# Sums of the FFN-input weight quarters: accumulating DMAs in DRAM instead of additions on GpSimd

## The chip, the cores and the metric

The kernel runs on one core of a Trainium2 chip. The core has a matrix engine (TensorE, PE in the profile, with its weight loads as PEld), VectorE (DVE), ScalarE (ACT), GpSimd (POOL) and SyncE (SP), which here only issues DMAs, beside 16 DMA engines. Each engine works through its own instructions in order, and engines wait for each other by semaphores. The metric is the time of one execution on the device in microseconds; lower is better. All arrays are float32.

## The reference, cut to what matters

The computation is one decoder block on a sequence of 1024 tokens with 1024 channels: a dilated attention and a causal convolution in parallel, merged by gates, and then a feed-forward part:

```python
h = rms_norm(x, g_pre_mix);  z = h @ w_in            # q, k, v, GLU input, two gates
y_attn = dilated_attention_mixer(q, k, v, ...)
y_conv = conformer_conv_mixer(glu_in, ...)           # GLU, depthwise conv of width 31, LN, swish, product
merged = sigmoid(z_ga) * y_attn + sigmoid(z_gc) * y_conv
x = x + rms_norm(merged @ w_mix_out, g_post_mix)
h = rms_norm(x, g_pre_ffn)
gate, up = split(h @ w_ffn_in)                       # 1024 x (2 x 2816)
x = x + rms_norm((silu(gate) * up) @ w_ffn_out, g_post_ffn)
```

The change concerns the weights of `h @ w_ffn_in`, and the sums of blocks of `h` for the same product.

## The kernel before, in words

**Precision.** Every float32 operand of a product is split into a rounded high part and the remainder. ScalarE writes the high part and VectorE (or GpSimd, where `wsplit` is set to it) the low part: `part` and `both` (L208 the copy, L209 the subtraction), `split` (L1337, L1338), `two_weights.split` (L1897, L1898). A product is three matmuls: high with high, high with low, low with high. In `unit` (L318 to L320) and `prod` (L334 to L336) these are 128 x 512.

**Order.** The program is written out by hand. TensorE's products call `tick` once for every step of the contraction, which is three full-width matmuls. Work for the other engines hangs on these ticks: generators registered with `bg` go on by one step per tick, and a yielded number makes them pause that many ticks; `later` and `when` put single steps on a tick. So the ticks set where an instruction stands in its engine's queue, and the semaphores then set when it runs. An engine whose queue is empty ahead of an instruction runs it early, long before the tick's own time on TensorE.

**Stages.** `start` (L565 to L595) loads x and three weights, normalizes and makes the first products (L629) while the rows arrive. Up to about 100 us come single GLU jobs; up to about 560 us pairs of weight tiles (GLU, gates, queries and keys) with one level of a Strassen-Winograd scheme: seven products for eight, from sums of weight quarters that `quarters` has GpSimd make (L228, L229, L235, L236) and from sums of h's blocks. A pair's weights are loaded at L177 through SyncE, 2 ticks into the pair ahead, and their split begins at tick 18. In the same stages the convolution runs on VectorE (L759), with `phases` (L728) on GpSimd. Values, attention, the merge and the output product follow up to about 1090 us, the FFN input up to about 1500, the FFN output up to the end.

**The FFN-input stage.** The first two of 22 column tiles are plain. The other 20 use a Winograd scheme on two levels. For each tile five products of the outer level are made directly (`("one", m, i)`: A11, S1, S2, S4, S3), and the two others are done for pairs of tiles with a second level, seven half-width products per group of two tiles (`("two", g, n)`, L2150 to L2152); there are ten groups. `line` is the order of all of them on TensorE, and `put` gives each its tick.

The weight sums of a tile are `S1 = A21 + A22`, `S2 = S1 + A11`, `S3 = A11 + A21`, `S4 = S2 + A12`. `one_weights` loads the four quarters of tile m by two DMAs (L1853, L1854), 18 ticks ahead; GpSimd makes the sums in SBUF (L1859, L1860, L1868, L1875); ScalarE and VectorE split them. `two_weights` makes the second level's sums in the same way from the quarter that both levels keep (L1923, L1924, L1928, L1932), four additions a group.

The moving operands of the second level are sums of blocks of h. `fourth_sums` and `eighth_sums` make them, half 0 before and half 1 in the first tile of the stage: two subtractions on GpSimd (L427, L428), the rest on VectorE, splits at L421 and L422, and a store to the DRAM tiles `d_t` (L423). `moving_load` (L1947) reads them back, two 512 KB tiles for each product, ahead of its use; those of products 1 and 5 are kept. Results are spilled to DRAM through L1954 (`spill`) for the FFN output. L2059 to L2070 finish the products of a tile, L2080 to L2095 those of a group; L2050 copies the first product of a tile out of PSUM. All these loads and spills stand in SyncE's one queue, in the order of the program.

Of the kernel before, what the change touches and what calls it, by code (L numbers as in the profile page):

```python
# [18 lines left out]
H = 512  # L19
# [43 lines left out]
class Build:  # L63
# [346 lines left out]
    def eighth_sums(self, e, low, given, dst):  # L410
# [16 lines left out]
        nc.gpsimd.tensor_tensor(t1, b11, b12, op=OP.subtract)  # L427
        nc.gpsimd.tensor_tensor(t3, b22, b12, op=OP.subtract)  # L428
# [1070 lines left out]
def build(ctx, tc, aps):  # L1499
# [39 lines left out]
    B.d_t = {(n, e): B.dram.tile([128, 1024], F32, name=f"dt{n}{e}") for n in range(7) for e in range(2)}  # L1539
    B.d_att = {(g, hp): B.dram.tile([128, T], F32, name=f"datt{g}{hp}") for g in range(3) for hp in range(4)}  # L1540
# [4 lines left out]
    def u_out(j, x):  # L1545
        nc.sync.dma_start(B.d_u[j], x)
        B.un = j + 1

# [24 lines left out]
    qs = B.bg(B.quarter_sums(xs, (h[0][:4], h[0][4:], h[1][4:])))  # L1573
    h = xs = None
# [268 lines left out]
    Wj, Yj, Qj, out2, parts, moving = {}, {}, {}, {}, {}, {}  # L1843
    gadd = nc.gpsimd.tensor_tensor

    def one_weights(m):
# [4 lines left out]
        def load():  # L1851
            st["X"], Yj[m] = B.ring(), B.slot()
            nc.sync.dma_start(st["X"], aps["w_f2"][m, 0])  # L1853
            nc.sync.dma_start(Yj[m], aps["w_f2"][m, 1])  # L1854

        def s12():
            x, y, n = st["X"], Yj[m], B.ring()
            st["N"] = n
            gadd(n[:, L], x[:, R], y[:, R], op=OP.add)  # L1859
            gadd(n[:, R], n[:, L], x[:, L], op=OP.add)  # L1860

        def a11():
            x = B.split(st["X"][:, L], H)
            w["A11"] = x[:, L], x[:, R]

        def s3():
            x = st["X"]
            gadd(x[:, R], x[:, L], x[:, R], op=OP.add)  # L1868

        def split12():  # L1870
            h, l = B.both(st["N"])
            w["S1"], w["S2"] = (h[:, L], l[:, L]), (h[:, R], l[:, R])

        def s4():
            gadd(st["X"][:, L], st.pop("N")[:, R], Yj[m][:, L], op=OP.add)  # L1875
# [8 lines left out]
    def halves(y):  # L1884
        return y.rearrange("p (e k n) -> p k e n", e=2, k=2)
# [4 lines left out]
    def two_weights(g):  # L1890
        a = [2 * g, 2 * g + 1]
        st = {}

        def split(n, x):
# [472 lines left out]
```

## Time and profile before

| | |
|---|---|
| median of 3 runs | 1725.92 us (1725.79 to 1732.4) |
| the profiled execution | 1719.96 us, its span 1717.8 us |
| TensorE busy | 1678.9 us, 98% of the span |
| VectorE, ScalarE, GpSimd busy | 1318.9, 850.3, 693.8 us |
| DMA traffic | 345.32 MB, mean 201 GB/s |
| of it on GpSimd's own queue | 352 packets, 0.18 MB |

Busy time is given per engine and per stretch of the span. A matmul's shown duration overlaps the next one's; the spacing of their starts is what TensorE needs. The lists of waits name an engine's instruction, what released it, and the total, number and longest of such waits. In an operation, `b<-d,b` names the tiles written and read without their numbers. Lines of DMAs give the issue; the landing times are listed apart. The granted clock of TensorE is 1.00 at full speed.

### The profile page before, as it was taken

The numbers are of one execution on the slowest core, as the hardware profiler recorded it, in microseconds if no ns is written. First come the engines' busy times: TensorE is split into PE (matmuls) and PEld (weight loads), VectorE is DVE, ScalarE is ACT, GpSimd is POOL, SyncE is SP. The second block draws the span as 40 slices with busy tenths as digits, with TensorE's granted clock in tenths as the row PEclk, the third lists the DMA queues.
The fourth block names the chain that finished last, engine by engine and source line by source line (L and its number), as shares of the span: only waits on it lengthen the run. The fifth ranks groups of instructions, "written<-read, shape, count | busy, mean of one in ns | idle before, by whom it ended". The sixth has DMA issues, their size and how long they took to land.

```text
span 1717.8 us, 24884 instructions
## 1 busy us (share of the span) xinstructions
PE 1678.9 (98%) x8527; PEld 1415.6 (82%) x8527; DVE 1318.9 (77%) x2238; ACT 850.3 (49%) x1676; POOL 693.8 (40%) x523
## 2 busy tenths in 40 slices
PE   9999999999999999999999999879999999999998
PEld 7788888888888899998888888668888888888886
DVE  6789978889998778788876656857676766777686
ACT  6344343444444688888522467333443344364463
POOL 0017778887885456565101301234434544200000
PEclk9999999999999999999999999989999999999999
DMA  4342434445567897889987424286666656795234
GB/s 165 115 172 90 157 117 141 156 175 180 168 183 205 251 274 219 246 238 273 319 277 260 166 87 172 92 317 247 239 248 232 248 215 228 258 363 163 101 133 153
DMA packets 180762, 345.32 MB, mean 201 GB/s; under 512 B 49185, under 2 KB 82460, under 8 KB 180636
## 3 DMA queue, kind: packets, MB, share of 16 engines
q1 hardware_dynamic: 180140, 343.29, 59.7%
q8 instruction: 67, 1.10, 0.3%
q14 instruction: 59, 0.48, 0.1%
q0 software_dynamic: 352, 0.18, 0.1%
q10 hardware_dynamic: 144, 0.26, 0.0%
HBM read 245.63 MB, written 102.76 MB: 203 GB/s over the span
## 4 chain that ended last, share of the span: by engine, by line
PE 38%; DVE 6%; issue 3%; ACT 3%; DMA 2%; SPq 0%; POOL 0%; DVEq 0%; ACTq 0%; POOLq 0%
PE p L2249 12%; PE p L1749 5%; PE p L334 3%; PE p L335 3%; PE p L336 3%; PE p L318 3%; PE p L319 3%; PE p L320 3%; PE p L2152 2%; PE p L2150 2%; PE p L2151 1%; DVE b L2089 1%; ACT b L208 1%; DVE b L1338 1%; DMA b<-dt 1%
## 5 line engine op out<-in xcount | busy, mean ns | idle before, releaser
L336 PE MATMUL p<-b,b 128*128 128x512 f32 x1044 | 407.7, 391 | 8.4 <-DVE b L209 6.6
L334 PE MATMUL p<-b,b 128*128 128x512 f32 x1044 | 408.2, 391 | 3.6 <-ACT b L2050 3.1
L335 PE MATMUL p<-b,b 128*128 128x512 f32 x1044 | 407.6, 390 | 0.0
L336 PEld LDWEIGHTS p<-b,b 128*128 128x128 f32 x1044 | 196.3, 188 | 53.8 <-DVE b L209 10.3
L334 PEld LDWEIGHTS p<-b,b 128*128 128x128 f32 x1044 | 196.6, 188 | 44.6 <-ACT b L2050 4.0
L335 PEld LDWEIGHTS p<-b,b 128*128 128x128 f32 x1044 | 196.6, 188 | 38.2
L2249 PE MATMUL p<-b,b 128*128 128x512 f32 x924 | 209.6, 389 | 0.0
L2249 PEld LDWEIGHTS p<-b,b 128*128 128x128 f32 x924 | 173.4, 188 | 36.0
L759 DVE SCALAR_TENSOR_TENSOR p<-b,par,p 128x511 f32<-128x511 f32 (+14 forms) x232 | 163.5, 739 | 0.0
L318 PE MATMUL p<-b,b 128*128 128x512 f32 x368 | 146.9, 399 | 0.0
L1017 PE MATMUL p<-b,b 128*128 128x512 f32 x384 | 144.1, 407 | 0.0
L320 PE MATMUL p<-b,b 128*128 128x512 f32 x368 | 143.5, 390 | 0.0
L319 PE MATMUL p<-b,b 128*128 128x512 f32 x368 | 143.5, 390 | 0.0
L209 POOL TENSOR_TENSOR b<-d,b 128x1024 fp32r<-128x1024 f32 x44 | 106.9, 2429 | 79.7 <-ACT b L208 72.4
L1859 POOL TENSOR_TENSOR d<-d,b 128x512 f32<-128x512 f32 x20 | 26.2, 1308 | 233.9 <-DMA b<-w_f 188.6
L208 ACT CAST b<-d 128x1024 fp32r<-128x1024 f32 x86 | 90.2, 1049 | 59.3 <-POOL d L229 55.1
L1338 DVE TENSOR_TENSOR b<-b,b 128x512 fp32r<-128x512 f32 x129 | 94.2, 733 | 21.9 <-ACT b L1337 20.4
L1018 PE MATMUL p<-b,b 128*128 128x256 f32 x384 | 107.7, 280 | 0.0
L1337 ACT CAST b<-b 128x512 fp32r<-128x512 f32 x129 | 79.9, 619 | 47.5 <-PE p L2249 18.1
L1146 ACT ACTIVATE c<-c,stat 128x128 f32<-128x128 f32 (+1 forms) x192 | 85.2, 448 | 13.4 <-DVE stat L1136 11.9
L2150 PE MATMUL p<-b,b 128*128 128x256 f32 x280 | 79.7, 285 | 11.8 <-DMA b<-dt 8.7
L1749 PE MATMUL p<-b,b 128*128 128x512 f32 x384 | 89.4, 391 | 0.0
(271 smaller groups left out, 3591.9 us busy)
## 6 DMA issues: line engine op xcount, KB each, us to landing
b<-dt SPq DMA_DIRECT2D x104, 512.0 KB, 5.4
b<-w_in SPq DMA_DIRECT2D x30, 512.0 KB, 4.9
dk<-c SPq DMA_DIRECT2D x48, 256.0 KB, 4.2
dq<-c SPq DMA_DIRECT2D x48, 256.0 KB, 3.5
b<-dq SPq DMA_DIRECT2D x48, 256.0 KB, 4.8
b<-dk SPq DMA_DIRECT2D x48, 256.0 KB, 7.0
d<-w_in SPq DMA_DIRECT2D x23, 512.0 KB, 4.0
b<-w_fo SPq DMA_DIRECT2D x44, 256.0 KB, 5.4
```

What stands on the lines that cost most here:

```text
L318: nc.tensor.matmul(ps, hi[:, s], a, start=kt == 0, stop=False)
L319: nc.tensor.matmul(ps, hi[:, s], b, start=False, stop=False)
L320: nc.tensor.matmul(ps, lo[:, s], a, start=False, stop=kt == nk - 1)
L334: nc.tensor.matmul(ps, hi[:, s], a, start=first and kt == 0, stop=False, skip_group_check=True)
L335: nc.tensor.matmul(ps, hi[:, s], b, start=False, stop=False, skip_group_check=True)
L336: nc.tensor.matmul(ps, lo[:, s], a, start=False, stop=kt == 3, skip_group_check=True)
L759: nc.vector.scalar_tensor_tensor(A[i][:, j:], src[i][:, :H - j], w[i], A[i][:, j:], op0=OP.mult, op1=OP.add)
L1017: nc.tensor.matmul(ps, a, w, start=kt == 0, stop=kt == KT - 1, skip_group_check=True)
L1338: nc.vector.tensor_tensor(s[:, 512:512 + n], src, f(s[:, :n]), op=OP.subtract)
L1749: nc.tensor.matmul(banks[tt][nh], st, wt[:, nh * H:(nh + 1) * H], start=bool(kt == 0 and a), stop=bool(kt == KT - 1 and b))
L2150: nc.tensor.matmul(o, hi, a, start=new, stop=False, skip_group_check=True)
L2249: nc.tensor.matmul(acc[t], x, y, start=first and e == 0, stop=last and e == 2, skip_group_check=True)
```

## The change

Before the stages with pairs a new generator, `weight_sums`, is registered. It makes all weight sums of both levels in DRAM, for all 20 tiles at once: one DMA copies one operand into the DRAM tile of the sum, a second one adds the other operand to it (`accum_op`). There are eight sums, so 16 DMAs, issued from GpSimd's queue and 45 ticks apart. The four sums of the outer level have 20 x 128 x 512 floats, the four of the inner level half of that.

In the FFN-input stage GpSimd does nothing any more. `one_weights` loads A11 and the four ready sums, each 128 x 512, in two steps; `two_weights` loads each of its seven weights by a DMA of its own, 17 ticks ahead of use and 10 ahead of its split. Both then only split. The host stores the weights as quarters (`w_l1`, `w_l2`) instead of tiles with two quarters each (`w_f2`).

The two subtractions of `eighth_sums` move to VectorE. In the order of the products, the first group's products each come after a later product of tile 2, and the finish of h's sums is called one product earlier; in the last tile the group's product 3 comes one product earlier, and the step that takes its result out of PSUM is held until the tile's last product is done.

```diff
@@ eighth_sums
-        nc.gpsimd.tensor_tensor(t1, b11, b12, op=OP.subtract)
-        nc.gpsimd.tensor_tensor(t3, b22, b12, op=OP.subtract)
+        nc.vector.tensor_tensor(t1, b11, b12, op=OP.subtract)
+        nc.vector.tensor_tensor(t3, b22, b12, op=OP.subtract)
@@ build
+    n1, n2 = (FT - PLAIN) * 128, (FT - PLAIN) * 64
+    B.d_s1 = {n: B.dram.tile([n1, H], F32, name=f"ds{n}") for n in ("S1", "S2", "S3", "S4")}
+    B.d_s2 = {n: B.dram.tile([n2, H], F32, name=f"de{n}") for n in ("s1", "s2", "s3", "s4")}
...
+    def weight_sums():
+        def flat(x):
+            return x.rearrange("(a r) n -> a (r n)", r=4)
+        def raw(x):
+            return x.rearrange("m p n -> (m p) n")
+        add = {"accum_op": OP.add, "max_dma_last_dim": 8192}
+        a11, a12, a21, a22 = (raw(aps["w_l1"][i]) for i in range(4))
+        b11, b12, b21, b22 = (raw(aps["w_l2"][i]) for i in range(4))
+        S, s = B.d_s1, B.d_s2
+        for d, x, y in ((S["S1"], a21, a22), (s["s1"], b21, b22), (S["S2"], S["S1"], a11), (s["s2"], s["s1"], b11),
+                        (S["S3"], a11, a21), (s["s3"], b11, b21), (S["S4"], S["S2"], a12), (s["s4"], s["s2"], b12)):
+            nc.gpsimd.dma_start(flat(d), flat(x))
+            yield 44
+            nc.gpsimd.dma_start(flat(d), flat(y), **add)
+            yield 44
...
     qs = B.bg(B.quarter_sums(xs, (h[0][:4], h[0][4:], h[1][4:])))
+    B.bg(weight_sums())
@@ the order of the products
         if m == 2:
-            after = {0: (0,), 1: (1,), 2: (2, 3), 3: (4, 5), 4: (6,)}
+            after = {1: (0,), 2: (1,), 3: (2, 3), 4: (4, 5, 6)}
...
-            after = {1: (0,), 2: (1,), 3: (2,), 4: (3, 4, 5, 6) if m == FT - PLAIN - 1 else ()}
+            after = {1: (0,), 2: (1,), 3: (2, 3) if m == FT - PLAIN - 1 else (2,), 4: (4, 5, 6) if m == FT - PLAIN - 1 else ()}
@@ one_weights (the loads of w_f2 and the additions s12, s3, s4 are gone)
+        def load(x, name, c):
+            nc.sync.dma_start(x, aps["w_l1"][0, m] if name == "A11" else B.d_s1[name][m * 128:(m + 1) * 128])
+        def load12():
+            st["A11"], st["N"] = B.half(), B.slot()
+            load(st["A11"], "A11", 0)
+            load(st["N"][:, L], "S1", 0)
+            load(st["N"][:, R], "S2", 0)
+        def load34():
+            x = st["X"] = B.slot()
+            load(x[:, L], "S4", 0)
+            load(x[:, R], "S3", 0)
...
-        for n, step in ((-18, load), (-9, s12), (-7, a11), (-5, s3), (-3, split12), (0, s4), (5, split34)):
+        for n, step in ((-19, load12), (-8, a11), (-11, load34), (-4, split12), (4, split34)):
@@ two_weights (the additions s12, s3, s4 are gone)
+        def load(n):
+            x = st[n] = B.half()
+            i = {0: 0, 1: 1, 6: 3}.get(n)
+            nc.sync.dma_start(x, B.d_s2[{2: "s2", 3: "s1", 4: "s3", 5: "s4"}[n]][g * 128:(g + 1) * 128] if i is None
+                              else aps["w_l2"][i, g])
+        def split(n):
+            parts[g, n] = B.split(st.pop(n), H)
         for n in range(7):
+            t = at["two", g, n]
+            when(t - 17, lambda n=n: load(n))
+            when(t - 7, lambda n=n: split(n))
@@ the loop over line
-            if m == 0 and i == 2:
+            if m == 0 and i == 1:
                 B.finish(qs)
...
+            if i == 4 and held:
+                held.pop(3)()
...
-            two_done(g, n, ps)
+            if (g, n) == (GROUPS - 1, 3):
+                held[3] = lambda ps=ps: two_done(g, 3, ps)
+            else:
+                two_done(g, n, ps)
```

More of the change, by code (lines that the diff above doesn't have):

```diff
@@ L1841, in when @@
         B.plan.setdefault(max(tick, B.ticks + 1), []).append(step)
[L1843 to L1844 removed]
+    Wj, Qj, out2, parts, moving = {}, {}, {}, {}, {}
     def one_weights(m):
@@ L2340 @@
     wf = tiles(g["w_ffn_in"][0], 8).reshape(2, FT, 128, 1024)
+    wq = wf[:, PLAIN:].reshape(2, FT - PLAIN, 128, 2, H).transpose(0, 3, 1, 2, 4)
+    w2 = wq[:, 1].reshape(2, -1, 2, 128, 2, 256).transpose(2, 4, 1, 3, 0, 5)
     arrays = {
```

64 lines of the change are left out of this document (4 added, 60 removed).

## The prediction

> **What bounds the kernel now.** First the page, then the busy time by stretch, then the waits of TensorE. The page:
>
> ```profile
> span 1717.8 us, 24884 instructions
> PE 1678.9 (98%) x8527; PEld 1415.6 (82%) x8527; DVE 1318.9 (77%) x2238; ACT 850.3 (49%) x1676; POOL 693.8 (40%) x523
> ```
>
> TensorE is busy 98% and idle 38.9 us (1717.8 - 1678.9). No change that leaves the products alone can gain more than that. The same by stretch; columns are the stretch, its length, busy time with instructions of PE, PEld, DVE, ACT, POOL, then the granted clock, the DMA engines' busy share and GB/s:
>
> ```profile
> 0.00:100.00 100.00, 98.46 (x425) 76.20 (x426) 74.97 (x105) 52.24 (x76) 1.99 (x7) 1.00 0.43 157
> 100.00:560.00 460.00, 459.55 (x2032) 379.27 (x2031) 406.02 (x556) 191.43 (x284) 337.08 (x191) 1.00 0.49 156
> 1090.00:1160.00 70.00, 54.65 (x261) 45.16 (x260) 47.47 (x52) 24.69 (x41) 27.52 (x18) 0.93 0.63 242
> 1160.00:1500.00 340.00, 328.19 (x1777) 281.56 (x1776) 239.24 (x289) 139.16 (x223) 142.72 (x101) 1.00 0.66 241
> ```
>
> From 100 to 560 us (the GLU, gate and query/key pairs) TensorE loses 0.45 us in 460: nothing to win there, only to lose. The FFN-input stage, 1090 to 1500, loses 70 - 54.65 = 15.35 and 340 - 328.19 = 11.81 us, together 27.2. That is the ceiling of what the change can win. What ended those idle times (total us, times, longest):
>
> ```profile
> PE p L2150 <- DMA b<-dt: 8.7, 1, 8.7
> PE p L336 <- DVE b L209: 6.6, 8, 1.6
> PE p L2152 <- DVE b L1898: 3.8, 9, 0.5
> PE p L334 <- ACT b L2050: 3.1, 2, 2.0
> PE p L2150 <- DVE b L2080: 2.0, 1, 2.0
> PE p L336 <- DVE b L1338: 1.9, 1, 1.9
> PE p L2150 <- ACT b L1897: 1.1, 1, 1.1
> ```
>
> One wait of 8.7 us for h's block sums out of DRAM (`d_t`), and many short ones for VectorE, mostly for the low part of the split weights (L209, L1898).
>
> **Part 1: GpSimd's sums leave the FFN stage.** Removed are 4 additions for each of 20 tiles and 4 for each of 10 groups, 120 in all, nearly all in this window's GpSimd time (first row); GpSimd itself waits there for the loaded quarters (second row), so it isn't the bound. What it costs is paid by VectorE. Three rows of the timelines (start, duration), the first two the same operation on VectorE without and beside GpSimd, the third what GpSimd ran:
>
> ```profile
> 1090.00:1500.00 410.00, 170.25 (x118) 0.99 0.65 241
> ...
> POOL d L1859 <- DMA b<-w_f: 188.6, 18, 13.8
> ...
> 1100.57 0.68 DVE L1781 TENSOR_TENSOR c<-c,c 128x512 f32<-128x512 f32 x1
> 1103.44 1.78 DVE L1786 TENSOR_TENSOR c<-c,c 128x512 f32<-128x512 f32 x1
> ...
> 1104.64 1.75 POOL L428 TENSOR_TENSOR c<-b,b 128x512 f32<-128x512 f32 x1
> ```
>
> A VectorE operation with two operands in SBUF takes 1.78 us beside GpSimd and 0.68 alone, so each meeting costs about 1.1. Without the additions the short waits should fall. Of the 27.2 us those for VectorE or ACT are 27.2 - 8.7 = 18.5; 6.6 of these (both waits for L2050 and L1338, and the longest for L209) belong to the stage's first 30 us, 11.9 to the steady part. I take half of each as GpSimd's doing, -3 and -6; bounds 0 and -18.5. The Trainium skill, "SBUF — State Buffer", section "Who interferes with whom", says that a VectorE instruction with two SBUF inputs contends with a GpSimd instruction that reads SBUF; these rows agree, with 1.78 against 0.68 us.
>
> **Part 2: h's block sums on VectorE, and the first group one product later.** `eighth_sums` runs twice, so VectorE gets 4 subtractions more, by L1781's row 4 x 0.68 = 2.7 us, two of them ahead of the stage and two in its start. For the group's first product, the place of the 8.7 us:
>
> ```profile
> 1128.30 0.39 PE L335 MATMUL p<-b,b 128*128 128x512 f32 x1
> 1128.53 0.39 PE L336 MATMUL p<-b,b 128*128 128x512 f32 x1
> 1137.64 0.55 PE L2150 MATMUL p<-b,b 128*128 128x256 f32 x1 [8.72 <-DMA b<-dt]
> 1140.34 0.63 PE L334 MATMUL p<-b,b 128*128 128x512 f32 x1
> 1140.76 0.63 PE L335 MATMUL p<-b,b 128*128 128x512 f32 x1
> ...
> 1131.81 1.63 DVE L2070 TENSOR_TENSOR c<-c,c 128x512 f32<-128x512 f32 x1
> ...
> 1133.88 7.86 SPq L1947 DMA_DIRECT2D b<-dt x12
> ```
>
> Tile 1 ends at 1128.53, but the `dt` loads stand in SyncE's queue behind the spill of the sum at L2070, which ends at 1133.44 (1131.81 + 1.63), so they issue at 1133.88 and the first pair lands 3.6 us later, 1137.5. In the change TensorE first does products 0 and 1 of tile 2: 24 matmuls of 0.23 us (start to start, 1128.30 to 1128.53; 0.227 over many) are 5.4 us, so it comes for the group at 1134.2. With VectorE about 2 us earlier at the spill the pair lands at 1135.5: 1.3 us of wait are left, a gain of 7.4. After the wait matmuls start 0.42 us apart instead of 0.227; some six of these and twelve half-width ones cost 2.3 us, gone too if the wait is short. Part 2 then gives -9.7 + 0.7 (the subtractions, half hidden) = -9; bounds -11 (the wait gone) and 0 (the loads no earlier). The last group's product 3 moves ahead of tile 19's last one; both are in the line anyway: 0, and at worst the 2.0 us of L2150 <- L2080 again.
>
> **Part 3: more loads in the stage.** A tile's two 512 KB loads become five of 256 KB (`A11` and four sums), and seven of 256 KB a group are new. A group of two tiles loaded 4 x 512 KB of weights and 10 x 512 KB of `dt` and spilled 7 x 256 KB, 8.75 MB with 21 issues; now it is 4.25 + 5 + 1.75 = 11 MB with 34. The stage's 0.66 becomes about 0.66 x 11/8.75 = 0.83. Median times to landing:
>
> ```profile
> b<-dt SPq DMA_DIRECT2D x104, 512.0 KB, 5.4
> d<-w_f SPq DMA_DIRECT2D x20, 512.0 KB, 5.2
> b<-w_f SPq DMA_DIRECT2D x20, 512.0 KB, 6.5
> ```
>
> A group's weight is issued 10 ticks ahead of its split, and a tick is three full-width matmuls, 0.68 us: 6.8 us of room against 5.2 to 6.5. Where a load is late, ACT waits with PSUM copies behind it, and the split leaves 7 ticks, 4.8 us, before TensorE asks. 70 such weights, a few late past that: +5, bounds 0 and +12.
>
> **Part 4: the accumulating DMAs beside the first stages.** Sixteen DMAs on GpSimd's queue, one every 45 ticks (30.6 us). Each of S1 to S4 is 20 x 128 x 512 x 4 B = 5.24 MB, copied once and added to once; the halves s1 to s4 are 2.62. No step of any engine waits for them before the FFN stage, but GpSimd issues them in order, and an addition waits for its copy. Their price: a DRAM-to-DRAM copy exists already, `rep`:
>
> ```profile
> 57.14 0.77 SPq L529 DMA_DIRECT2D rep<-line x1
> ...
> 62.00:68.00 6.00, 6.00 (x28) 4.99 (x27) 2.90 (x3) 1.95 (x3) 0.00 (x0) 1.00 0.53 201
> ```
>
> 201 GB/s at a share of 0.53 is 379 GB/s at 1.0, so a large copy is 13.8 us of all engines and a small one 6.9. An addition also reads its target: between 13.8 and twice that, 27.6. All sixteen take between 4 x (13.8 + 6.9) x 2 = 166 and 248 us of engine time in some 490 us whose share is 0.49 already: 0.83 to 1.0.
>
> Now where they land. The first copy waits for nothing, and what stands ahead of it on GpSimd is only the table's load; today GpSimd then sits until 88.98 us:
>
> ```profile
> 1.31 0.64 POOL L516 DMA_DIRECT2D c<-p_tab x1 [0.46 <-issue]
> 88.98 1.03 POOL L728 TENSOR_TENSOR c<-b 128x512 f32<-128x512 f32 x1 [87.03 <-DMA b<-du]
> ...
> 12.95 1.15 ACT L603 ACTIVATE b<-b,gains 128x1024 fp32r<-128x1024 f32 x1 [2.72 <-DMA b<-xT]
> 15.48 0.74 PE L629 MATMUL p<-b,b 128*128 128x512 f32 x2 [0.30 <-DVE b L604]
> ...
> 2.00:21.00 19.00, 18.65 (x70) 12.56 (x69) 10.70 (x14) 13.36 (x22) 0.00 (x0) 1.00 0.96 367
> 21.00:44.00 23.00, 23.00 (x114) 19.34 (x114) 18.87 (x31) 15.03 (x21) 0.00 (x0) 1.00 0.01 4
> ```
>
> So it issues at 2 us, not beside a later stage but into the load of x and the first weights, when the DMA engines are 0.96 busy, and not in the 23 us after it, when they are idle. At 12.95 ACT waits for x, and TensorE is hardly ahead of it (0.30 us idle at 15.48): a late x is late at the end. Lower bound 0, if the loads go first. Shared by bytes, the 3.1 MB up to x's third tile (three of x and three weights, 0.52 each) take at half of 367 GB/s until 19 us instead of 12.9: +6. If each engine does a whole 64 KB row of the copy (80 rows of 16384 floats, by the build) for each 1 to 4 KB row of a load, the loads stand for the 13.8 us of the copy: upper bound. With rows so unequal I take a value near that, +11. The Trainium skill, "DMA: Bandwidth & Descriptors", section "Queues, rings and completion order", says that an engine takes turns between queues packet by packet; by that the result is the upper bound if a long row is one packet, and no row here shows two full queues.
>
> In the pairs a weight has this much room:
>
> ```profile
> 316.66 0.38 SPq L177 DMA_DIRECT2D d<-w_in x1
> 331.61 1.05 ACT L208 CAST b<-d 128x1024 fp32r<-128x1024 f32 x1
> ...
> d<-w_in SPq DMA_DIRECT2D x23, 512.0 KB, 4.0
> ...
> 483.00:560.00 77.00, 76.81 (x345) 62.62 (x344) 68.10 (x83) 34.26 (x51) 50.91 (x28) 1.00 0.67 186
> ```
>
> 14.95 us from issue to split against 4.0 to landing, so 10.9 of slack; behind the split stand ACT's PSUM copies and GpSimd's L209. A copy's 13.8 us leaves at most 3 us of it uncovered, and only when it meets the load. An addition of up to 27.6 us is longer than the slack; shared by bytes it halves the loads' rate, and where the share is 0.67 (483 to 560) the backlog is 0.67 x 27.6 - 13.8 = 5 us, inside the slack. Starved by long rows it is 27.6 - 10.9 = 17 us, for three large additions at worst 50. I take +9, nearer to sharing; bounds 0 and 50.
>
> **The sum.** -3 - 6 - 9 + 5 + 11 + 9 = +7 us. The profiled execution took 1719.96 us (span 1717.8 and 2.16 around it), which gives 1727; the runs' median is 1725.92, 6 above it, so the median of the changed kernel is 1733 by the sum. Since the terms of part 4 reach further up than down and those of part 1 are guesses of one half, I put the forecast at +10: 1736 us.
>
> **Rivals.**
> - Faster: the loads go ahead of the copies. Then part 4 is 0 or little, and -3 - 6 - 9 + 5 = -13 stays: 1713. For it: the FFN stage's 27.2 us are real, and SyncE's loads have 10.9 us of slack in the pairs. Against it: 0.96 share at the start, with TensorE 0.30 us behind the data. It decides when the start loses less than 4 us.
> - Even: sharing by bytes, +6 at the start and +3 in the pairs, against -11 in the FFN stage (-13, with 2 us more of late loads): 1724.
> - GpSimd's queue: an addition waits on GpSimd for its copy; if an addition takes over 61 us, the next small copy behind it is late and GpSimd, 337 of 460 us busy in the pairs, holds L209 for TensorE. At 20 us an instance and three of them: 1786.
> - It doesn't do what it says: the FFN stage is not shortened, because ACT waits for the new loads (+12) as long as VectorE did, while part 4 stays: 1750.
>
> **How the numbers follow.** Chances: the forecast's case (start near the row-by-row bound) 0.40, faster 0.22, even 0.22, GpSimd's queue 0.08, no gain in the stage 0.08. About 0.5%, 8.6 us, is what a measurement can tell from no change. Slower by that: 0.40 less a third that ends within it, with the two last, and a few hundredths of even: 0.45; faster: 0.22 and a part of even, 0.28; within: 0.27. The range leaves out a tenth at each end: 1711 (the faster case in full) to 1768 (half of the queue's case); the forecast's own range is 1726 to 1755.
>
> **What would show it.** At the start: L629's products after 14 us late by 6 to 14 us, with ACT's L603 waiting for xT, and the first copy's bytes in GpSimd's queue from 2 us on; if L603 waits no longer than 2.72, that term is wrong. In the pairs, waits of ACT's L208 for w_in, and of TensorE for ACT. In the FFN stage, no GpSimd time, L2150's wait near 1 us, DVE's L209 waits gone; new waits of ACT for the sums if part 3 counts. The prediction falls if TensorE is not idle in the first 25 us, or if the additions take far over 30 us.

## The result, and the profile after

The changed kernel takes 1816.8 us (median of 4 runs, 1815.41 to 1818.03), the kernel before on the same chip 1729.16 (4 runs, 1725.79 to 1735.01). The ratio is 1.0503 [1.0467, 1.0539]: 5% slower, outside the predicted range of 1711 to 1768. The page of the changed kernel (its profiled execution took 1815.71 us), engines and DMA queues:

```profile
span 1813.9 us, 24918 instructions
PE 1705.7 (94%) x8527; PEld 1430.5 (79%) x8527; DVE 1267.4 (70%) x2242; ACT 849.8 (47%) x1676; POOL 524.0 (29%) x415
...
q1 hardware_dynamic: 198860, 366.89, 60.5%
q0 software_dynamic: 5024, 63.10, 13.8%
```

GpSimd lost 170 us of work and VectorE 51.5, as meant; GpSimd's own DMA queue, 0.18 MB before, moves 63.10 MB and holds the 16 DMA engines for 13.8% of the span, 250 us. TensorE was idle 38.9 us and is now idle 108.2, which is 69.3 of the 96.1 us by which the span grew. The other 26.8 are in its busy time (1678.9 to 1705.7 us, for the same 8527 matmuls); a place where matmuls start further apart after a long wait follows below.

Where the time went is read from the first start of four of TensorE's lines: the pairs (L334), the values behind them (L1017), the transposes ahead of the FFN input (L1479), the FFN output (L2236, before L2249). The rows, by line, give the first and the last start. Before:

```profile
L334 PE MATMUL p<-b,b x1044: 387/389/628, 110.6 to 1492.6; 128*128 128x512 f32 x174
L1017 PE MATMUL p<-b,b x384: 389/397/793, 549.9 to 776.9; 128*128 128x512 f32 x192
L1479 PE MATMUL p<-ident,b x64: 270/272/332, 1006.8 to 1069.0; 128*128 128x128 f32 x64
L2249 PE MATMUL p<-b,b x924: 388/389/397, 1501.2 to 1710.4; 128*128 128x512 f32 x185
```

After:

```profile
L334 PE MATMUL p<-b,b x1044: 387/389/797, 148.2 to 1587.0; 128*128 128x512 f32 x174
L1017 PE MATMUL p<-b,b x384: 387/397/793, 644.7 to 880.1; 128*128 128x512 f32 x192
L1479 PE MATMUL p<-ident,b x64: 270/272/328, 1110.6 to 1172.8; 128*128 128x128 f32 x64
L2236 PE MATMUL p<-b,b x924: 388/389/400, 1597.4 to 1806.6; 128*128 128x512 f32 x185
```

| stage | before, us | after, us | difference | predicted |
|---|---|---|---|---|
| up to the pairs | 110.6 | 148.2 | +37.6 | +11 |
| pairs | 439.3 | 496.5 | +57.2 | +9 |
| values, attention, merge, output product | 456.9 | 465.9 | +9.0 | 0 |
| FFN input | 494.4 | 486.8 | -7.6 | -13 |
| FFN output to the end | 216.6 | 216.5 | -0.1 | 0 |

The sum is 96.1 us, the difference of the spans. The profiled execution of the kernel before lies 6 us under the median of the first runs, so these differences together are some 8 us more than that of the medians (87.6); in which stage that execution was quicker the profile doesn't say.

**The start.** The timeline of the changed kernel, chosen rows of GpSimd, ScalarE and TensorE (start, duration, then the idle time before and what ended it), and the stretches:

```profile
1.97 0.56 POOL L1567 DMA_DIRECT2D dsS<-w_l  x1
22.11 1.14 POOL L1569 DMA_DIRECT2D dsS<-w_l  x1 [19.58 <-DMA dsS<-w_l]
...
22.04 0.72 ACT L603 ACTIVATE b<-b,gains 128x512 fp32r<-128x512 f32 x1 [17.21 <-DMA b<-xT]
...
33.10 1.15 ACT L603 ACTIVATE b<-b,gains 128x1024 fp32r<-128x1024 f32 x1 [7.00 <-DMA b<-xT]
...
22.81 10.31 PE L629 MATMUL p<-b,b 128*128 128x512 f32 x35 [17.14 <-ACT b L603]
```

```profile
2.00:22.00 20.00, 3.68 (x9) 1.19 (x7) 1.09 (x2) 1.68 (x4) 0.53 (x1) 1.00 0.98 327
22.00:56.00 34.00, 24.98 (x91) 17.88 (x91) 13.20 (x18) 13.65 (x19) 1.14 (x1) 1.00 1.03 270
```

The copy issues at 1.97 us and has landed by 22.1, when GpSimd's wait for it ends. Of the 6.5 MB moved in these 20 us (327 GB/s) it is 5.24; x and the weights got the other 1.3, a fifth, and ScalarE waits 17.2 us for x. Then the addition issues straight behind and lands 36.3 us later, at about 58 us: of the 9.2 MB moved from 22 to 56 us it is 5.1 and the loads are 4.1, 44%. ScalarE waits for x again, 7.0 us.

**The pairs.** What ended TensorE's idle times (total, times, longest):

```profile
PE p L334 <- ACT c L348: 33.5, 6, 12.7
PE p L629 <- ACT b L603: 20.3, 3, 17.1
...
PE p L2134 <- ACT b L1337: 4.8, 2, 2.6
...
PE p L336 <- POOL b L209: 4.1, 6, 1.5
PE p L2134 <- DMA b<-dt: 3.5, 2, 2.4
PE p L2134 <- DVE b L2062: 3.5, 1, 3.5
```

L348 is ScalarE's copy of a finished product out of PSUM. In the pairs it waits for a buffer whose store to DRAM isn't finished. Such waits of ScalarE and VectorE, and ScalarE's for the pairs' weights:

```profile
ACT c L348 <- DMA dk<-c: 27.7, 4, 16.0
DVE c L907 <- DMA dk<-c: 19.7, 3, 12.5
ACT c L895 <- DMA dk<-c: 14.6, 2, 12.9
...
ACT b L208 <- DMA d<-w_in: 5.7, 4, 2.2
```

From 148.2 to 644.7 us, the pairs, TensorE is idle 43.3 us, and 33.5 of these end with L348:

```profile
148.20:644.70 496.50, 453.17 (x1934) 367.19 (x1933) 391.05 (x535) 181.86 (x271) 342.91 (x204) 0.96 0.81 235
```

One of these places in SyncE's and TensorE's timelines:

```profile
561.37 4.10 SPq L886 DMA_DIRECT2D dk<-c  x2
567.29 19.76 SPq L886 DMA_DIRECT2D dq<-c  x2
587.14 0.79 SPq L177 DMA_DIRECT2D d<-w_in  x1
...
587.82 0.80 PE L334 MATMUL p<-b,b 128*128 128x512 f32 x1 [12.71 <-ACT c L348]
```

Behind this wait of 12.7 us TensorE's matmuls start 0.43 us apart until 593.5 us and 0.23 apart afterwards (their rows aren't shown), which costs some 2.7 us more than the wait itself. Over the pairs the granted clock is 0.96, where it was 1.00.

The DMAs from 555 to 590 us, by queue (packets, MB, share) and by issue:

```profile
q0 software_dynamic: 656, 5.24, 74.7%
q1 hardware_dynamic: 5720, 2.57, 27.5%
...
dsS<-w_l POOLq DMA_DIRECT2D x1, 5120.0 KB, 30.9
...
dk<-c SPq DMA_DIRECT2D x4, 256.0 KB, 25.7
```

An addition (L1569) issues at 555.7 and lands 30.9 us later. In this stretch its queue has 74.7% of the DMA engines, all other transfers 27.5%, and a `dk` store takes 25.7 us; its median on the page is 4.2 us before and 17.5 after. SyncE itself is held: two issues last 19.76 us together, one of them 16.3 by the line's maximum below, and the weights' loads at 587.14 stand behind them. ScalarE is held little by these loads, though, 5.7 us in all by the rows above. The rows of that line (minimum, median, maximum of one issue in ns), before and then after:

```profile
L886 SPq DMA_DIRECT2D dq<-c x32: 513/546/3499, 412.6 to 560.4; - x32
```

```profile
L886 SPq DMA_DIRECT2D dq<-c x32: 512/798/16316, 482.6 to 665.1; - x32
```

**The FFN input.** Two windows that answer to those of before, the first again from just ahead of the stage's first product (1194.72 us) and 70 us long, and a third inside the second:

```profile
1194.00:1264.00 70.00, 59.46 (x281) 48.90 (x281) 41.36 (x60) 27.19 (x44) 0.00 (x0) 0.95 0.82 308
1264.00:1596.00 332.00, 324.80 (x1759) 281.50 (x1758) 197.41 (x281) 135.28 (x218) 0.00 (x0) 0.99 0.84 304
...
1260.00:1578.00 318.00, 316.61 (x1705) 273.56 (x1703) 187.52 (x266) 129.69 (x206) 0.00 (x0) 1.00 0.86 310
```

The first loses 10.5 us where it lost 15.4, the second 7.2 where it lost 11.8. Between the first groups and the last one almost nothing is lost any more: 1.4 us in 318, where 320 us of the kernel before (1160 to 1480) lost 9.4. Most of what is left in the second window is the last group, whose weights come late. SyncE's load, ScalarE's split of it, and TensorE:

```profile
1573.96 1.04 SPq L1912 DMA_DIRECT2D c<-des  x2
...
1579.61 0.62 ACT L1337 CAST b<-c 128x512 fp32r<-128x512 f32 x1 [9.40 <-DMA c<-des]
...
1580.28 0.58 PE L2134 MATMUL p<-b,b 128*128 128x256 f32 x1 [2.65 <-ACT b L1337]
```

### The profile page after: what moved, and what is told of

It reads as the page before. It is cut to its first block, busy times and chain, and to the rows that moved or that the text cites. A ratio compares the mean times of both kernels' runs of the same rounds, so it can differ in the third digit from the quotient of the medians.

```text
span 1813.9 us, 24918 instructions
## 1 busy us (share of the span) xinstructions
PE 1705.7 (94%) x8527; PEld 1430.5 (79%) x8527; DVE 1267.4 (70%) x2242; ACT 849.8 (47%) x1676; POOL 524.0 (29%) x415
## 3 DMA queue, kind: packets, MB, share of 16 engines
q0 software_dynamic: 5024, 63.10, 13.8%
## 4 chain that ended last, share of the span: by engine, by line
PE 56%; DMA 10%; DVE 6%; ACT 3%; issue 2%; POOL 1%; SPq 1%; DVEq 0%; ACTq 0%; POOLq 0%
PE p L2236 12%; PE p L1017 5%; DMA dk<-c 5%; PE p L334 5%; PE p L335 5%; PE p L336 5%; PE p L1773 4%; PE p L318 3%; PE p L320 3%; PE p L319 3%; PE p L1018 2%; PE p L1133 2%; PE p L1204 2%; PE p L2136 2%; PE p L1171 2%
## 5 line engine op out<-in xcount | busy, mean ns | idle before, releaser
L334 PE MATMUL p<-b,b 128*128 128x512 f32 x1044 | 414.5, 397 | 40.9 <-ACT c L348 33.5
L336 PE MATMUL p<-b,b 128*128 128x512 f32 x1044 | 411.1, 394 | 4.6 <-POOL b L209 4.1
L335 PE MATMUL p<-b,b 128*128 128x512 f32 x1044 | 411.8, 394 | 0.0
L334 PEld LDWEIGHTS p<-b,b 128*128 128x128 f32 x1044 | 199.1, 191 | 86.9 <-ACT c L348 36.6
L336 PEld LDWEIGHTS p<-b,b 128*128 128x128 f32 x1044 | 198.9, 191 | 50.5 <-POOL b L209 7.3
L335 PEld LDWEIGHTS p<-b,b 128*128 128x128 f32 x1044 | 199.4, 191 | 39.0
L2236 PE MATMUL p<-b,b 128*128 128x512 f32 x924 | 209.6, 389 | 0.0
L2236 PEld LDWEIGHTS p<-b,b 128*128 128x128 f32 x924 | 173.4, 188 | 36.0
L1338 DVE TENSOR_TENSOR b<-c,b 128x512 fp32r<-128x512 f32 x175 | 119.9, 687 | 64.3 <-ACT b L1337 64.1
L1017 PE MATMUL p<-b,b 128*128 128x512 f32 x384 | 146.6, 413 | 5.6 <-DVE b L202 5.6
L1337 ACT CAST b<-c 128x512 fp32r<-128x512 f32 x175 | 107.9, 618 | 93.9 <-DMA c<-des 39.5
L318 PE MATMUL p<-b,b 128*128 128x512 f32 x368 | 146.9, 399 | 0.0
L320 PE MATMUL p<-b,b 128*128 128x512 f32 x368 | 143.5, 390 | 0.0
L319 PE MATMUL p<-b,b 128*128 128x512 f32 x368 | 143.5, 390 | 0.0
L209 POOL TENSOR_TENSOR b<-d,b 128x1024 fp32r<-128x1024 f32 x44 | 106.0, 2409 | 102.4 <-ACT b L208 78.0
L1338 DVE TENSOR_TENSOR b<-b,b 128x512 fp32r<-128x512 f32 x129 | 89.8, 698 | 26.5 <-ACT b L1337 24.8
L208 ACT CAST b<-b 128x1024 fp32r<-128x1024 f32 x67 | 70.2, 1047 | 81.2 <-POOL b L236 45.4
L2134 PE MATMUL p<-b,b 128*128 128x256 f32 x280 | 80.8, 289 | 14.3 <-ACT b L1337 4.8
## 6 DMA issues: line engine op xcount, KB each, us to landing
dk<-c SPq DMA_DIRECT2D x48, 256.0 KB, 17.5
```

The lines of the kernel that those rows point to most:

```text
L318: nc.tensor.matmul(ps, hi[:, s], a, start=kt == 0, stop=False)
L319: nc.tensor.matmul(ps, hi[:, s], b, start=False, stop=False)
L320: nc.tensor.matmul(ps, lo[:, s], a, start=False, stop=kt == nk - 1)
L334: nc.tensor.matmul(ps, hi[:, s], a, start=first and kt == 0, stop=False, skip_group_check=True)
L335: nc.tensor.matmul(ps, hi[:, s], b, start=False, stop=False, skip_group_check=True)
L336: nc.tensor.matmul(ps, lo[:, s], a, start=False, stop=kt == 3, skip_group_check=True)
```

## The experiments

In one table, each against the kernel before: the ratio of the times, and how much longer each stage of the profiled execution is than before (from the same four rows as above).

| kernel | us | ratio | start | pairs | values to output product | FFN input |
|---|---|---|---|---|---|---|
| the change | 1816.8 | 1.0503 [1.0467, 1.0539] | +37.6 | +57.2 | +9.0 | -7.6 |
| no sum DMAs | 1713.3 | 0.9916 [0.9890, 0.9943] | +1.2 | -0.1 | +1.5 | -8.4 |
| order only | 1724.49 | 0.9982 [0.9969, 0.9995] | +0.5 | -0.1 | +0.4 | +3.4 |
| no sums, old order | 1709.64 | 0.9898 [0.9880, 0.9916] | +0.7 | -0.1 | +2.9 | -11.0 |
| no sums, output's loads later | 1709.56 | 0.9911 [0.9881, 0.9940] | +0.7 | -0.1 | 0.0 | -11.5 |
| copies only | 1749.17 | 1.0128 [1.0104, 1.0152] | +18.7 | +18.3 | +3.0 | -6.4 |
| sums after the start | 1794.35 | 1.0385 [1.0360, 1.0411] | +7.0 | +67.0 | +6.1 | -8.8 |
| copies in 8 KB rows | 1801.76 | 1.0423 [1.0402, 1.0445] | +28.4 | +49.2 | +10.0 | -5.4 |
| all in 2 KB rows | 1770.36 | 1.0249 [1.0228, 1.0270] | +15.1 | +32.4 | +8.9 | -7.4 |
| 2 KB rows, after the start | 1775.5 | 1.0274 [1.0257, 1.0291] | +4.5 | +48.7 | +8.7 | -8.0 |
| the same in pieces, one DMA in 10 ticks | 1755.46 | 1.0178 [1.0152, 1.0205] | +0.7 | +41.0 | +1.3 | -9.6 |
| in pieces, 15 ticks | 1756.74 | 1.0164 [1.0142, 1.0185] | +0.9 | +10.1 | +30.8 | -6.8 |
| in pieces, 22 ticks | 1747.45 | 1.0128 [1.0096, 1.0160] | +0.2 | +3.8 | +35.1 | -11.0 |

**No sum DMAs.** The changed kernel with the 16 DMAs left out; raw quarters are loaded in the sums' place, with the same bytes and number of loads.

```diff
-    B.bg(weight_sums())
...
-            nc.sync.dma_start(x, aps["w_l1"][0, m] if name == "A11" else B.d_s1[name][m * 128:(m + 1) * 128])
+            nc.sync.dma_start(x, aps["w_l1"][{"A11": 0, "S1": 2, "S2": 3, "S3": 1, "S4": 2}[name], m])
...
-            nc.sync.dma_start(x, B.d_s2[{2: "s2", 3: "s1", 4: "s3", 5: "s4"}[n]][g * 128:(g + 1) * 128] if i is None
-                              else aps["w_l2"][i, g])
+            nc.sync.dma_start(x, aps["w_l2"][{2: 3, 3: 2, 4: 1, 5: 2}[n] if i is None else i, g])
```

> The changed kernel without the sixteen DMAs of the sums; the stage loads raw quarters of the same size in place of the sums, so its number of loads and bytes stays and its result is not the block's. Theory A (the sums' DMAs displace the transfers of the first stages, 37.6 us up to the first pair and 57 us in the pairs by the trace of the change): the first pair begins at 110.6 us as before, the pairs end at 550, and what is left is the FFN stage with its -8.6 at the start and about +1 after it: 1721 us. Rival B (something else of the change, such as the new weight layout or the loads, costs in the early stages): over 1750 us.

Measured 0.9916 [0.9890, 0.9943], 14.5 us faster than before (0.0084 x 1727.58, the median beside it). Start and pairs are those of the kernel before within 1.2 us. So the whole loss belongs to the 16 DMAs, and the rest of the change is worth what the terms of parts 1 to 3 add up to, -13.

**Sums after the start.** The generator is registered where the pairs begin; its first copy issues at 90.6 us, not at about 120, and so still falls into the end of the start.

```diff
-    B.bg(weight_sums())
...
     def beside():
...
         B.bg(conv)
+        B.bg(weight_sums())
```

> The changed kernel with the sums' DMAs registered where the pairs begin, so that the first copy stands behind the convolution's first addition on GpSimd and goes out at about 120 us instead of 2 us. Theory A1 (the start's 37.6 us is a collision with the load of x, where TensorE has no reserve): the first pair begins at 111 us, the two DMAs cost some 6 us more in the pairs, 1785 us. Rival B1 (each DMA costs its engine time wherever it stands, some 13 and 26 us): the start is whole, the pairs lose 57 + 38, total unchanged within 10 us of 1817.

The start comes back but for 7.0 us; the pairs lose 67 instead of 57. 22 us of the 88 are won, not 37: a part of what the start paid is only moved. In this run SyncE's longest stretch of two `dq` issues is 25.36 us, behind an addition issued 4.9 us ahead of it.

**Copies only.** The eight additions are left out, so the "sums" are copies of one operand.

```diff
             nc.gpsimd.dma_start(flat(d), flat(x))
             yield 44
-            nc.gpsimd.dma_start(flat(d), flat(y), **add)
             yield 44
```

> The changed kernel with the eight copies but without the eight additions (the sums are then only copies, and the result is not the block's). If the long rows of the copies are what starves the loads: the start still loses 17 us (ACT's wait for the second half of x's first tile), the pairs lose most of their 57 us, 1780 us or more. If it is the engine time in all, of which the additions hold the larger part: start +18, pairs +10, FFN -8: 1750 us.

1749.17, in total as expected, but the pairs lose 18.3 us and not 10. GpSimd's queue then shows (span 1751.4 us):

```profile
q0 software_dynamic: 1056, 31.64, 5.4%
```

5.4% is 95 us for the copies, so the additions hold the engines for 250 - 95 = 155 us: a large copy 15.8 us, a large addition 26 (each set is worth six large ones). The copies cost the start 18.7 and the pairs 18.3; the additions cost another 18.9 and 38.9. This split takes the copies to hold the engines as long with the additions as without them.

**Copies in 8 KB rows, and all in 2 KB rows.** The bytes stay; only the length of a row changes. In the change the large copies go in 64 KB rows (the small in 40 KB), additions in 8 KB rows. The second edit asks for 2 KB rows; in its trace the additions go in packets of 2 KB, but the copies in packets of 4 KB (the first copy: 1327 packets for 5.25 MB).

```diff
-            nc.gpsimd.dma_start(flat(d), flat(x))
+            nc.gpsimd.dma_start(flat(d), flat(x), max_dma_last_dim=8192)
```

```diff
-        add = {"accum_op": OP.add, "max_dma_last_dim": 8192}
+        add = {"accum_op": OP.add, "max_dma_last_dim": 2048}
...
-            nc.gpsimd.dma_start(flat(d), flat(x))
+            nc.gpsimd.dma_start(d, x, max_dma_last_dim=2048)
...
-            nc.gpsimd.dma_start(flat(d), flat(y), **add)
+            nc.gpsimd.dma_start(d, y, **add)
```

> The changed kernel with the copies in rows of 8 KB, as the additions have them, instead of 64 and 40 KB. In the trace of the change the loads of the start got 20% of the bytes beside the 64 KB copy (2 to 22 us) and about 43% beside the 8 KB addition (22 to 56 us). Theory A2 (row length sets the share that the loads get): the loads get 2.8 MB by 22 us instead of 1.3, ACT's first wait for x falls from 17 us to under 8, the start loses 30 us instead of 37.6, the pairs a few less: 1805 us. Rival B2 (only the engine time counts, the row length does not): 1817 us within 4, ACT's first wait still 17 us.

> The changed kernel with copies and additions in rows of 2 KB. Theory A2 (the share goes by row length): the loads, in rows of up to 4 KB, get more than half beside both; the start loses 20 us instead of 37.6, the pairs 35 instead of 57: 1777 us. Rival B2 (engine time): the sums cost no less engine time in short rows, the loads wait as long in all: 1810 us or more.

Both come out 3 to 7 us better than the numbers expected. ScalarE's waits for x in the start, by line (idle before, and what ended it), of the change and then with 2 KB rows:

```profile
L603 ACT ACTIVATE b<-b,gains 128x1024 fp32r<-128x1024 f32 (+1 forms) x9 | 9.5, 1052 | 40.6 <-DMA b<-xT 40.6
```

```profile
L603 ACT ACTIVATE b<-b,gains 128x1024 fp32r<-128x1024 f32 (+1 forms) x9 | 9.4, 1049 | 15.3 <-DMA b<-xT 15.3
```

40.6 us become 15.3, and the pairs lose 32 instead of 57. While the first copy runs, the other queues get 18% of the engines' time beside 64 KB rows (2 to 21.4 us), 33% beside 8 KB rows (2 to 23.8) and 52% beside packets of 4 KB (2 to 31.6). So the length of the rows sets how much of the engines the loads get: about half of the loss is this.

**Order only.** The kernel before, GpSimd's additions and all, with the two subtractions on VectorE, the new order of tile 2 and the earlier finish.

```diff
-        nc.gpsimd.tensor_tensor(t1, b11, b12, op=OP.subtract)
-        nc.gpsimd.tensor_tensor(t3, b22, b12, op=OP.subtract)
+        nc.vector.tensor_tensor(t1, b11, b12, op=OP.subtract)
+        nc.vector.tensor_tensor(t3, b22, b12, op=OP.subtract)
...
-            after = {0: (0,), 1: (1,), 2: (2, 3), 3: (4, 5), 4: (6,)}
+            after = {1: (0,), 2: (1,), 3: (2, 3), 4: (4, 5, 6)}
...
-            if m == 0 and i == 2:
+            if m == 0 and i == 1:
```

> The kernel before with only two parts of the change: the four subtractions of h's block sums on VectorE, and the first group's products one product later in tile 2 (with the finish of h's sums one product earlier). If the wait of 8.7 us for the block sums falls by the order alone: about -8 us, 1720 us with before at 1728, and the short waits for VectorE stay. If it falls by VectorE's freedom from GpSimd's additions: at most -3 us.

3.1 us faster than before by the medians (0.0018 x 1727.58), with 0.9 to 5.4 by the interval; the profiled stage shows no gain. Of the kernels that do the whole computation it is the only one below the kernel before, by less than the half per cent that a measurement can tell.

**No sums, with the old order of tile 2.** Here and in the next one, "no sums" is the first experiment's kernel, which leaves the sums out of the computation.

```diff
-            after = {1: (0,), 2: (1,), 3: (2, 3), 4: (4, 5, 6)}
+            after = {0: (0,), 1: (1,), 2: (2, 3), 3: (4, 5), 4: (6,)}
...
-            if m == 0 and i == 1:
+            if m == 0 and i == 2:
```

> The kernel without the sums' DMAs (as e1_no_sum_dmas, so the result is not the block's), with tile 2's old order: the group's products each one product earlier, and the finish of h's sums at the third product. Together with e1_no_sum_dmas (both, ratio 0.9916) and e6_order_only (order alone, 0.9982) it tells the order from VectorE's relief. If the order is worth its 9 us once VectorE is relieved: 1722 us. If the relief alone brings the spill and the loads forward: 1715 us.

17.6 us faster than before; beside the 14.5 with the new order the intervals overlap (14.5 to 20.7 and 9.8 to 19.0). Once GpSimd's additions are out, no gain of the order can be told.

**No sums, the FFN output's first loads later.** These loads stand on SyncE ahead of the last group's late weights.

```diff
-            if m == FT - PLAIN - 1 and i == 0:
+            if m == FT - PLAIN - 1 and i == 2:
```

> The kernel without the sums' DMAs (raw quarters in place of the sums, as in e1_no_sum_dmas, so the result is not the block's), with the first five pairs of loads for the FFN output issued at the last tile's third product instead of its first. In the change they stand ahead of the last group's weights in SyncE's queue, ACT waits 9.4 us for these, and the last group loses about 8 us by the trace. Theory C: 1706 us against 1713 of e1_no_sum_dmas, the wait of ACT's L1337 for the last group's weights under 2 us. Rival: the FFN output's first product then waits for its loads instead, 1713.

0.9911 beside 0.9916: no gain that can be told, and ScalarE's wait for the last group's weights stays at 9.4 us. Loading those weights a tile earlier would be the direct test; it wasn't tried. So what makes the last group late stays open.

**2 KB rows, after the start.** Both edits above together.

> The changed kernel with both edits that helped by themselves: the generator registered only with the pairs, and copies and additions in rows of 2 KB instead of 64 and 8 KB. Theory A (row length sets the share that the loads get, and the start and the pairs lose separately): the start as in the kernel before within 4 us, the pairs 30 to 40 us longer instead of 57, values and attention +9, the FFN input -8: 1728 + 2 + 35 + 9 - 8 = 1766 us, or a little below. Rival B (row length helped only the start, where copy and x collide): the pairs stay 60 to 67 us longer, as with the later start alone, 1790 us or more.

A miss for the sum of the two: 1775.5 instead of 1766, and slower than 2 KB rows alone (1770.36). The start gives back 10.6 us and the pairs lose 16.3 more (48.7 against 32.4). Together start and pairs lose 53 against 47: the sums have to be done somewhere, and the start's DMA pauses (0.01 busy from 21 to 44 us before) were of use. This pointed to the total, not the place, which the pieces below test.

**In pieces.** 2 KB rows, after the start, each DMA cut into pieces of 640 rows (1.31 MB, 48 DMAs), one every 15, 10 or 22 ticks.

```diff
...
+            for r in range(0, d.shape[0], 640):
+                jobs.append((d[r:r + 640], x[r:r + 640], y[r:r + 640]))
+        for k in range(len(jobs) + 1):
+            if k < len(jobs):
+                d, x, y = jobs[k]
+                nc.gpsimd.dma_start(d, x, max_dma_last_dim=2048)
+                yield 14
+            if k:
+                d, x, y = jobs[k - 1]
+                nc.gpsimd.dma_start(d, y, **add)
+                yield 14
...
```

The kernels with 10 and 22 ticks also change two other pauses of 14 ticks by the same amount, one in the copies of the bias lines, up to the pairs, and one ahead of the first splits for the FFN output. The start (0.7 and 0.2 us longer than before) and the FFN output (216.6 and 216.5 us) don't show it; of the differences in the FFN input, -9.6 and -11.0 beside -6.8 with 15 ticks, a part may come from it.

> The same sums after the start and in 2 KB rows, but each of the 16 DMAs cut into pieces of 640 rows (1.31 MB): 24 copies and 24 additions, one every 15 ticks instead of one of 16 every 45 ticks, each copy issued before the addition of the piece ahead. The bytes stay the same. Theory A (a burst longer than the slack of a load, 10.9 us, is what TensorE pays for; a piece is 3.5 to 6 us of engine time): the pairs lose 0 to 10 us, the time is 1728 + 2 + 8 + 9 - 8 = 1739 us or less. Rival B (the bytes displace loads and stores whatever the burst): the pairs lose 30 us or more, as with rows of 2 KB uncut, 1760 to 1766 us.

> The pieces of 1.31 MB after the start again, one DMA every 10 ticks instead of 15, so that they end about 150 us earlier and well ahead of the values and attention. With one every 15 ticks the DMA engines were busy all the time from 200 to 640 us, the pairs lost 10 us, and 31 us were lost behind them, in values and attention. Theory A (the engine time of the sums, 15.4% of the span or 270 us, doesn't fit beside the loads and stores there, and a backlog is paid wherever it stands): the loss moves from values and attention into the pairs: pairs 25 to 40 us longer, values to merge 0 to 12 longer, in all 1750 to 1768 us. Theory B (what costs in values and attention is that sums run beside it, and short bursts cost the pairs little): pairs about +12, values to merge +5 or less, 1737 us.

> The same pieces, one DMA every 22 ticks, so that the sums spread from the pairs over values, attention and merge, to about 900 us. Theory A (backlog): the share of the DMA engines falls under 1.0 in the pairs, which lose 5 us or less; from 560 to 900 us the share was 0.83 to 0.96 in the kernel before, so 20 us or more are lost there: 1740 to 1752 us. Theory B (sums beside values and attention cost more than in the pairs): 40 us or more there, 1765 us or more.

With 15 ticks the pairs lose 10 us, the short bursts' promise, but 31 us are lost behind them, which neither theory had: 1756.74 against 1739. With 10 ticks the sums are all issued by 489 us, values and attention are almost as before, and the pairs lose 41; with 22 ticks it is the other way round. Both come out as the backlog theory had them, but for the 41 us where it said 40 at most. The stretches 110 to 560 and 560 to 700 us, with 10, 15 and 22 ticks (the last two columns are the share of the DMA engines and GB/s):

```profile
110.00:560.00 450.00, 423.04 (x1802) 345.05 (x1801) 369.28 (x506) 169.39 (x250) 350.71 (x227) 0.97 0.97 273
560.00:700.00 140.00, 139.50 (x841) 121.97 (x840) 108.62 (x188) 91.94 (x191) 73.79 (x66) 1.00 0.83 242
```

```profile
110.00:560.00 450.00, 443.57 (x1936) 363.14 (x1935) 395.94 (x537) 181.77 (x270) 367.37 (x232) 1.00 0.95 263
560.00:700.00 140.00, 118.58 (x715) 104.62 (x715) 79.77 (x159) 80.06 (x173) 59.19 (x60) 0.89 1.00 282
```

```profile
110.00:560.00 450.00, 445.36 (x1959) 365.95 (x1957) 394.70 (x540) 184.48 (x274) 357.43 (x218) 1.00 0.82 228
560.00:700.00 140.00, 128.12 (x826) 115.20 (x827) 90.70 (x204) 92.44 (x216) 65.93 (x70) 0.95 0.98 285
800.00:1010.00 210.00, 198.53 (x1005) 165.50 (x1003) 149.63 (x307) 93.45 (x243) 56.74 (x65) 0.98 1.03 320
```

Pairs and the stretch behind them lose together 42.3, 40.9 and 38.9 us. Before, three windows of the same stretches:

```profile
110.00:560.00 450.00, 449.55 (x1988) 370.99 (x1987) 396.42 (x541) 187.22 (x277) 337.08 (x191) 1.00 0.49 156
560.00:700.00 140.00, 139.42 (x968) 127.26 (x967) 106.72 (x265) 108.59 (x274) 77.03 (x84) 1.00 0.86 252
...
800.00:1010.00 210.00, 209.22 (x1020) 174.46 (x1019) 151.61 (x310) 93.61 (x228) 36.76 (x38) 1.00 0.74 243
```

Free engine time was 230 us up to 560 (0.51 x 450) and some 250 up to 700; the sums in 2 KB rows take 15.4% of the span, 270 us. With 10 and 15 ticks they don't fit, and the loss stands where the share comes to 0.95 and over: with 10 ticks in the pairs, with 15 behind them. With 22 ticks the last addition issues at 996 us, and up to 1010 some 320 us were free, so the total would fit; but the pairs then stay at 0.82 while the stages behind, with less to spare, are filled to 0.98 and 1.03, and lose there. This account is worked out from the shares; a spacing that goes by the free time of each stage would test it, and wasn't tried. Nor is a stage's mean share enough to foretell a loss: with 22 ticks the pairs have 0.82 and lose 3.8 us, and in the change they have 0.81 (148.2 to 644.7 us) and lose 57.2. There the sums come in DMAs of up to 5.24 MB that fill the engines for some 30 us at a time, as from 555 to 590 us.

The 9 us that the change itself lost behind the pairs are of this kind: its last addition issues at 636.3 us, 8 ahead of the values, and where the sums are done long before (10 ticks) that stretch loses 1.3.

## Why the prediction was wrong, step by step

**Right: the place and the sign of part 4.** The first copy does issue at 2 us into the load of x, ScalarE's L603 waits far longer than 2.72 us, TensorE waits in the pairs for ScalarE, and the FFN stage is shortened. The forecast had the right direction, +10 against +88.

**Wrong in size: the start, +11.** The term priced the first copy (13.8 us at most) and no more. The copy took 20 us to land (15.8 us of engine time by the copies alone, where the prediction had 13.8); the addition behind it, which the prediction priced for the pairs but not here, was issued by 22 us and lands at 58, into what was left of x's load. Copies alone cost 18.7, the additions as much again. Its bounds, 0 and 13.8, left a whole DMA out.

**Wrong in size: the pairs, +9.** The price of an addition was right: 26 us, inside 13.8 to 27.6, and all sixteen 250 us, at the end of 166 to 248. The step that failed is the one after it: each DMA was held against the slack of a single load, a weight's 10.9 us, under the word "shared by bytes". That slack mostly held: for `w_in` ScalarE's L208 waits 5.7 us in all and GpSimd's L228 14.0, 5.0 at most, and TensorE waits 4.1 us in all for GpSimd's L209. What broke is a transfer that the prediction gave no price, the `dk` stores. They land after 17.5 us in the median instead of 4.2, ScalarE's L348 waits 27.7 us for buffers that they hold, and 33.5 of the 43.3 us that TensorE is idle in the pairs end with L348. Sharing was unequal as well: beside an addition all other transfers got 27.5% of the engines (the row from 555 to 590 us), which is the starved case, whose 50 us the pairs even passed, and not the shared one. Nor did the term price what follows a wait, as part 2 does: of the 57.2 us 42.9 are idle time and 14.3 busy time (TensorE is busy for 438.9 us of the stage before and 453.2 after).

**Missed: values and attention, +9.** The term was not there; the sums were thought done with the pairs.

**Parts 1 to 3, -13: right as a sum, not in their shares.** Without the DMAs the kernel is 14.5 us faster [9.8 to 19], where the faster rival had 13. Part 2's -9 for the order fails as a cause: alone it gives 3.1 us, and without it the relief of VectorE gives 17.6. `L2150 <- DMA b<-dt` (8.7 us) did fall to 2.4 at most, and VectorE's L209 no longer stands among TensorE's longer waits in this kernel. But that wait is 5.5 us by the order alone and 5.2 by the relief alone, so each takes about 3 of its 8.7. The steady part of the stage gains 8 us (9.4 to 1.4), where part 1 had 6. Part 1's -9 was therefore too small and part 2's too large. Part 3's late loads are seen in two places: in the first group TensorE waits 2.2 us for a split that has itself waited 14.9 for `des`, and in the last one 2.65 us for the split and 3.5 for VectorE's L2062. That is inside the term's 0 to +12.

**The rivals.** "GpSimd's queue" gave 1786, the nearest number, by a mechanism that did not occur: GpSimd waited for a copy once, 19.6 us at the very start, and TensorE waited for GpSimd's L209 4.1 us in all. "Faster" and "even" needed a start that loses under 4 or 6 us. "Not shortened" is refuted by the FFN rows.

**What stays open.** Whether more buffers for the halves would have saved the pairs wasn't tried. It is shown that long rows and the spacing of the sums each count; that the held stores are the larger part of the pairs' loss rests on the waits above, and no run removes them alone. Why SyncE's issues last up to 16.3 us beside an addition is open too.

## What to carry to other kernels

Before moving work to DMAs, add up their engine time and set it against the free engine time of each stage they run beside, not against the slack of one load. Where the share comes near 1, be it for a single DMA of 30 us inside a stage with a lower mean, the engines that wait for other transfers pay; and look at all of these transfers, stores that hold buffers too. A DMA whose operands are ready at the beginning is issued as soon as its queue is empty, and so is what waits only for that DMA; price the chain, not its first link. Where bulk transfers must run beside small ones, use short rows and small pieces: here short rows halved the loss (88 to 42 us), and small pieces, issued later and further apart, brought it to 20.

## What the runs showed of the hardware that was not expected

- The share that loads get beside a bulk transfer goes with its rows: beside the same copy they got 18% of the engines' time with 64 KB rows, 33% with 8 KB rows and 52% with packets of 4 KB, and ScalarE's waits for x fall from 40.6 us to 27.4 and 15.3. The Trainium skill, "DMA: Bandwidth & Descriptors", section "Queues, rings and completion order", says that an engine takes turns between queues packet by packet; the direction agrees with it.
- Shorter rows cost more engine time in all (15.0% of the 2 KB run's span of 1767 us against 13.8% of 1814: 265 against 250 us) and still less time of the kernel.
- An accumulating DMA from DRAM to DRAM ran at 202 GB/s of engine time (31.5 MB in 155 us), a plain copy at 333 (31.6 MB in 95 us). The copies' longer rows don't explain it: with copies in 8 KB rows, like the additions, all sixteen take 247 us (13.7% of 1800), no more than the 250.
- SyncE can be held by the issue itself: one issue of a store took 16.3 us beside an addition, where the longest was 3.5 before.
- A wait of TensorE costs more than its length: behind one of 12.7 us the matmuls start 0.43 us apart instead of 0.23 for 5.7 us, and the granted clock of the pairs is 0.96 instead of 1.00. Of the 96.1 us by which the span grew, 26.8 are busy time; how much of it comes in this way wasn't added up.
